# A pad of 224 bytes behind the resident tokens of a two-layer transformer trunk

## The chip, the cores and the metric

The kernel runs on one core of a Trainium2 chip, in one launch. The metric is the device time in microseconds (us), the median over several runs. Engines are named as in the profile: PE is TensorE's matrix product, PEld its weight load, DVE is VectorE, ACT is ScalarE, POOL is GpSimd, and SP is the engine that issues the DMAs.

## The reference

512 tokens of 1024 channels pass through two layers. Each layer is a half FFN, a mixer, and another half FFN, each followed by a residual sum and a layer norm. The even layer's mixer joins an RG-LRU and an mLSTM, the odd one's an RWKV-7 and a gated linear attention. All is float32.

```python
alpha = DEEPNORM_ALPHA
for l in range(DEPTH):
    x = layer_norm(alpha * x + 0.5 * swiglu_ffn(x, ffn1_wi[l], ffn1_wo[l]), ln_g[l, 0], ln_b[l, 0])
    mix = even_mixer(x, ...) if l % 2 == 0 else odd_mixer(x, ...)
    x = layer_norm(alpha * x + mix, ln_g[l, 1], ln_b[l, 1])
    x = layer_norm(alpha * x + 0.5 * swiglu_ffn(x, ffn2_wi[l], ffn2_wo[l]), ln_g[l, 2], ln_b[l, 2])
```

`swiglu_ffn` multiplies the tokens by a matrix of 1024 x 5632, takes silu of one half times the other half, and multiplies the 2816 results by a matrix of 2816 x 1024. The mixers begin with projections of the tokens and end with a product of 1024 x 1024.

## The kernel before, in words

**Precision.** TensorE multiplies float32r operands in one pass. To keep float32's accuracy each operand is split into a high and a low part, both exact in float32r, and each product is done as three: high x high, low x high, high x low. The tokens stay in memory as `xh` and `xl`, transposed (128 channels of a group on the partitions, eight groups of 512 tokens along them).

**Streamed weights.** All weights come once, as a list of chunks of 512 KB, 128 partitions x 1024 float32. `load` (line 81) issues a chunk's DMA on SP into one of two `raw` buffers. `split` (line 89) makes `whi` (ACT, line 97) and `wlo` (DVE, line 99), in two halves of 512 columns; both have five buffers. `weights` (line 107) hands out the next chunk and keeps two more split and two more loading.

**Three kinds of products**, each of 24 matmuls with 512 moving columns a chunk:

```python
# project_T_steps, 121, 122, 125: weights stationary, tokens moving
mm(o, hi[:, kt, :n], self.xh[:, kt, t0:t1], ...)
mm(o, hi[:, kt, :n], self.xl[:, kt, t0:t1], ...)
mm(o, lo[:, kt, :n], self.xh[:, kt, t0:t1], ...)
# project_N_steps, 145 to 147: tokens stationary, weights moving
mm(acc[t], self.xh[:, k, ts], hi[:, z, :], ...)
mm(acc[t], self.xl[:, k, ts], hi[:, z, :], ...)
mm(acc[t], self.xh[:, k, ts], lo[:, z, :], ...)
# out_mm, 154 to 156: left operand (ah, al) stationary, weights moving
mm(o, ah, hi[:, cs], ...)
mm(o, al, hi[:, cs], ...)
mm(o, ah, lo[:, cs], ...)
```

**An FFN** (`ffn`, line 206) runs in two parts, of 12 and 10 groups of inner channels. Each group takes two chunks of the first matrix (results `pgu`, by `project_T`); their gated product is split into `hh` and `hl`, the inner tiles. Then the group's rows of the second matrix come, one chunk a group: `out_mm` with `hh`, `hl` on the left, into `acc`, for four tiles of 128 tokens and two halves of the columns. So an FFN has 44 input chunks and 22 output chunks; there are four FFNs. The first five input chunks of an FFN run in two token halves of 256 columns (48 matmuls a chunk in place of 24), because the last tokens come late from the step before.

**The mixers** (`even`, line 307; `odd`, line 554) use the same chunks and functions. Results named `pqk`, `prg`, `pgg` and `pj` come from `project_T`, `pv` and the chunk products named `po` from `project_N`, `pout` from `out_mm` (class `MixOut`). Even: 16 column chunks (four of them in token halves), 8 row chunks, 8 output chunks, four of which have tiles `qk` on the left and four `xh` and `xl`. Odd: 17 column chunks (four in token halves), 8 row chunks, 8 output chunks, all with `xh` and `xl`. Each has one more narrow chunk, in halves and without its own low part (16 matmuls in each half). In the odd mixer the large products are queued in fixed portions between small ones (a list of counts, `FILL`, written by hand), and the small ones wait in turn for DVE and ACT.

**Where things lie.** Tiles are allocated along a partition in the order of their pools, each start a multiple of 32 bytes. The pools `cp` (tokens, identity), `wp` (weights), `lp` (small ones) and then the pool of the stage stack up from the left; `x` (the residual, 16,384 bytes) and the odd mixer's work tiles lie at the right end.

```python
self.cp = E(tc.tile_pool(name="cp", bufs=1))
self.wp = E(tc.tile_pool(name="wp", bufs=1))
self.lp = E(tc.tile_pool(name="lp", bufs=1))
...
self.xh = self.cp.tile([P, 8, S], F32R, name="xh")
self.xl = self.cp.tile([P, 8, S], F32R, name="xl")
self.ident = self.cp.tile([P, P], F32, name="ident")
```

| tile | first byte of the partition | modulo 256 |
|---|---|---|
| `xh`, `xl` (16,384 bytes each) | 16,512 and 32,896 | 128 |
| `ident` (512), then `expo` (4) | 49,280 and 49,792 | 128 |
| `raw` (2 x 4,096) | 49,824 | 160 |
| `whi`, `wlo` (5 x 4,096 each) | 58,016 and 78,496 | 160 |
| `hh`, `hl` (13 x 2,048 each) | 100,256 and 126,880 | 160 |
| even mixer's `qk` (8 x 2,048) | 121,600 | 0 |
| even mixer's `u`, `wbd` | 177,760 and 109,280 | 96 and 224 |

Inside these tiles matmul operands start at steps of 512 or 2,048 bytes, so the last column holds for all of them.

## Time and profile before

| what | value |
|---|---|
| median of three runs | 2075.99 us (2074.61, 2075.99, 2079.17) |
| profiled execution: span from its first to its last instruction | 2075.2 us |
| profiled execution: its own time | not listed apart from the span |
| mean granted TensorE clock | 0.993 |
| matmuls (passes) | 10,485 |
| the four FFNs' share of the span | about 1,480 us |
| even mixer, odd mixer | about 225 and 352 us |

How to read it: a line such as "PE 2054.0 (99%) x10485" gives an engine's busy time, its share of the span, and its instructions. Matmuls are pipelined and their ends are modelled: one is listed with a duration of about 390 ns while the next one starts some 230 ns after it. So PE's busy share and the mean of a group say little on what a matmul costs. The differences of starts, in the timeline or in the chain that ended last, say it.

### The profile page before, as it was taken

The numbers are of one execution on the slowest core, as the hardware profiler recorded it, in microseconds if no ns is written. First come the engines' busy times: TensorE is split into PE (matmuls) and PEld (weight loads), VectorE is DVE, ScalarE is ACT, GpSimd is POOL, SyncE is SP. The second block draws the span as 40 slices with busy tenths as digits, with TensorE's granted clock in tenths as the row PEclk, the third lists the DMA queues.
The fourth block names the chain that finished last, engine by engine and source line by source line (L and its number), as shares of the span: only waits on it lengthen the run. The fifth ranks groups of instructions, "written<-read, shape, count | busy, mean of one in ns | idle before, by whom it ended". The sixth has DMA issues, their size and how long they took to land.

```text
span 2075.2 us, 26007 instructions
## 1 busy us (share of the span) xinstructions
PE 2054.0 (99%) x10485; PEld 1681.6 (81%) x10485; DVE 998.2 (48%) x1850; ACT 692.0 (33%) x1214; POOL 69.2 (3%) x128
## 2 busy tenths in 40 slices
PE   9999999999999999999999999999999999999998
PEld 8888888876888888888888888887778788888886
DVE  4332333766783323336432333578768674323335
ACT  4322332556433322322332232156324333322320
POOL 0000000100010000000000000000010200000001
PEclk9999999999999999999999999999899999999999
DMA  5223232321233223222332332241302023233231
GB/s 174 92 92 122 92 98 85 97 94 67 62 102 112 91 92 122 92 92 71 112 98 95 112 102 92 77 157 36 102 31 72 1 82 112 92 101 112 94 99 61
DMA packets 56456, 191.42 MB, mean 92 GB/s; under 512 B 7488, under 2 KB 7952, under 8 KB 56336
## 3 DMA queue, kind: packets, MB, share of 16 engines
q1 hardware_dynamic: 56336, 189.77, 28.6%
q8 instruction: 82, 1.34, 0.3%
q14 instruction: 38, 0.31, 0.0%
HBM read 185.55 MB, written 4.19 MB: 91 GB/s over the span
## 4 chain that ended last, share of the span: by engine, by line
PE 94%; DVE 4%; ACT 1%; issue 1%; DMA 1%; POOL 0%; POOLq 0%; DVEq 0%; SPq 0%; ACTq 0%
PE pgu L121 16%; PE pgu L125 16%; PE pgu L122 16%; PE acc L154 8%; PE acc L155 8%; PE acc L156 8%; PE pout L155 1%; PE pout L154 1%; PE pj L121 1%; PE pout L156 1%; PE pj L122 1%; PE pj L125 1%; PE pst L167 1%; PE pv L145 1%; PE pv L147 1%; PE pv L146 1%
## 5 line engine op out<-in xcount | busy, mean ns | idle before, releaser
L99 DVE TENSOR_TENSOR wlo<-raw,whi 128x512 fp32r<-128x512 f32 x658 | 426.0, 686 | 557.8 <-ACT whi L97 526.0
L97 ACT ACTIVATE whi<-raw 128x512 fp32r<-128x512 f32 x661 | 379.6, 623 | 845.2 <-PE pgu L122 409.0
L122 PE MATMUL pgu<-xl,whi 128*128 128x512 f32 (+1 forms) x1568 | 571.5, 373 | 0.0
L121 PE MATMUL pgu<-xh,whi 128*128 128x512 f32 (+1 forms) x1568 | 570.0, 372 | 1.5 <-ACT whi L97 1.2
L125 PE MATMUL pgu<-xh,wlo 128*128 128x512 f32 (+1 forms) x1568 | 361.3, 372 | 0.0
L121 PEld LDWEIGHTS pgu<-xh,whi 128*128 128x128 f32 x1568 | 293.5, 188 | 58.2 <-ACT whi L97 1.6
L122 PEld LDWEIGHTS pgu<-xl,whi 128*128 128x128 f32 x1568 | 294.3, 188 | 57.0
L125 PEld LDWEIGHTS pgu<-xh,wlo 128*128 128x128 f32 x1568 | 275.4, 188 | 56.8
L154 PE MATMUL acc<-whi,hh 128*128 128x512 f32 x704 | 274.5, 390 | 0.0
L155 PE MATMUL acc<-whi,hl 128*128 128x512 f32 x704 | 274.2, 390 | 0.0
L156 PE MATMUL acc<-wlo,hh 128*128 128x512 f32 x704 | 272.3, 390 | 0.0
L232 DVE TENSOR_TENSOR sg<-sg,pgu 128x512 f32<-128x512 f32 (+1 forms) x96 | 61.7, 643 | 348.4 <-PE pgu L125 344.7
L156 PEld LDWEIGHTS acc<-wlo,hh 128*128 128x128 f32 x704 | 132.2, 188 | 27.4
L154 PEld LDWEIGHTS acc<-whi,hh 128*128 128x128 f32 x704 | 132.2, 188 | 27.3
L155 PEld LDWEIGHTS acc<-whi,hl 128*128 128x128 f32 x704 | 132.2, 188 | 27.1
L159 ACT ACTIVATE hh<-sg 128x512 fp32r<-128x512 f32 (+1 forms) x96 | 57.3, 597 | 125.0 <-DVE sg L232 124.9
L231 ACT ACTIVATE sg<-pgu 128x512 f32<-128x512 f32 (+1 forms) x96 | 53.8, 562 | 59.3 <-PE pgu L125 58.8
L189 POOL TENSOR_SCALAR rs<-mv 128x1 f32<-128x1 f32 x24 | 13.2, 549 | 1536.3 <-DVE mv L187 1536.3
L159 ACT ACTIVATE xh<-pst 128x512 fp32r<-128x512 f32 x48 | 27.8, 597 | 109.0 <-PE pst L167 108.9
L121 PE MATMUL pj<-xh,whi 128*128 128x512 f32 (+2 forms) x184 | 62.4, 358 | 0.0
L160 DVE TENSOR_TENSOR hl<-sg,hh 128x512 fp32r<-128x512 f32 (+1 forms) x96 | 61.4, 640 | 0.5 <-ACT hh L159 0.5
L122 PE MATMUL pj<-xl,whi 128*128 128x512 f32 (+2 forms) x184 | 60.8, 348 | 0.0
(333 smaller groups left out, 1999.0 us busy)
## 6 DMA issues: line engine op xcount, KB each, us to landing
raw<-ffn_wi SPq DMA_DIRECT2D x176, 512.0 KB, 3.5
raw<-ffn_wo SPq DMA_DIRECT2D x88, 512.0 KB, 3.5
raw<-od_krv SPq DMA_DIRECT2D x12, 512.0 KB, 3.6
raw<-ev_qk SPq DMA_DIRECT2D x8, 512.0 KB, 3.7
raw<-ev_rg SPq DMA_DIRECT2D x8, 512.0 KB, 3.4
raw<-ev_w_out SPq DMA_DIRECT2D x8, 512.0 KB, 3.5
raw<-od_w_out SPq DMA_DIRECT2D x8, 512.0 KB, 3.7
x<-x SPq DMA_DIRECT2D x4, 512.0 KB, 6.0
```

Of the source, the lines that this page charges most:

```text
L97: self.nc.scalar.activation(hi[:, sl], t[:, sl], AF.Copy)
L99: self.nc.vector.tensor_tensor(out=lo[:, sl], in0=t[:, sl], in1=hi[:, sl].bitcast(F32), op=ALU.subtract)
L121: mm(o, hi[:, kt, :n], self.xh[:, kt, t0:t1], start=kt == 0, stop=False)
L122: mm(o, hi[:, kt, :n], self.xl[:, kt, t0:t1], start=False, stop=lo is None and kt == 7)
L125: mm(o, lo[:, kt, :n], self.xh[:, kt, t0:t1], start=False, stop=kt == 7)
L154: mm(o, ah, hi[:, cs], start=first and i == 0, stop=False)
L155: mm(o, al, hi[:, cs], start=False, stop=False)
L156: mm(o, ah, lo[:, cs], start=False, stop=last and i == len(lhs) - 1)
L159: self.nc.scalar.activation(hi, src, AF.Copy)
L160: self.nc.vector.tensor_tensor(out=lo, in0=src, in1=hi.bitcast(F32), op=ALU.subtract)
L231: nc.scalar.activation(sg, pp[f, 0][:, t0:t1], AF.Silu)
L232: nc.vector.tensor_tensor(out=sg, in0=sg, in1=pp[u][:, t0:t1], op=ALU.mult)
```

## The change

One tile of 56 float32 (224 bytes a partition) is allocated behind the identity matrix. Nothing reads it or writes it. Everything allocated after it on the left moves up by 224 bytes: `expo`, `raw`, `whi`, `wlo`, the small tiles, and the tiles of the FFNs and mixers. The other lines of the diff blank out comments; line numbers behind the pad rise by two.

```diff
         self.ident = self.cp.tile([P, P], F32, name="ident")
         nc.sync.dma_start(self.ident, a["c_ident"])
+
+        self.cp.tile([P, 56], F32, name="pad")
         self.expo = self.cp.tile([P, 1], F32, name="expo")
...
```

## The prediction

> **What bounds the kernel now.** I read the page's head first (which engine), then the view by stage (where), then the chain of waits and the timeline inside single stages (what one matmul costs there).

> ```profile
> span 2075.2 us, 26007 instructions
> ...
> PE 94%; DVE 4%; ACT 1%; issue 1%; DMA 1%; POOL 0%; POOLq 0%; DVEq 0%; SPq 0%; ACTq 0%
> ```

> 94% of the chain that ended last is TensorE itself. By stage (length, then busy time of PE, PEld, DVE, ACT, POOL, then the granted clock, the DMA engines' share and GB/s): a stage of input products of an FFN, one of its output products, the even mixer, the odd mixer.

> ```profile
> 212.00:323.90 111.90, 111.90 (x482) 90.09 (x481) 38.47 (x61) 36.25 (x62) 0.00 (x0) 1.00 0.31 99
> 147.00:211.90 64.90, 64.90 (x288) 53.73 (x287) 20.15 (x31) 12.71 (x22) 0.00 (x0) 1.00 0.33 106
> 381.00:606.00 225.00, 222.00 (x1104) 176.46 (x1102) 163.31 (x331) 116.29 (x191) 11.29 (x19) 1.00 0.27 85
> 1347.00:1698.60 351.60, 345.09 (x2429) 275.30 (x2428) 257.90 (x593) 140.54 (x268) 35.83 (x72) 0.97 0.21 66
> ```

> In the FFN stages PE never rests, at a granted clock of 1.00; in the mixers it rests 3.0 and 6.5 us. So the time is the number of matmuls times the spacing of their starts, and a change that touches no instruction can only act on that spacing. "Mean ns of one" doesn't give it, because matmuls overlap; the starts do. The chain in an input stage (start, length, what), one piece per chunk of streamed weights:

> ```profile
> 215.97 1.87 PE pgu L125 x8
> 221.57 1.87 PE pgu L125 x8
> 227.17 1.87 PE pgu L125 x8
> ```

> The same eight matmuls come back every 5.60 us. A chunk is 24 matmuls of 512 columns (eight on each of lines 121, 122, 125), so one starts every 5.60 / 24 = 0.2333 us. The chain in an output stage, first and last of 54 pieces:

> ```profile
> 159.88 0.23 PE acc L154
> ...
> 171.89 0.23 PE acc L156
> ```

> (171.89 − 159.88) / 53 = 0.2266 us. Both are single-pass products of 128 rows, 128 columns of weights and 512 moving columns, with PE never idle, yet one is 6.7 ns shorter. The timeline of the even mixer tells what doesn't make the difference: the output product there is the same function as the FFN's (lines 154 to 156), with other left operands.

> ```profile
> 583.79 0.39 PE L154 MATMUL pout<-whi,xh 128*128 128x512 f32 x1
> ...
> 586.35 0.39 PE L156 MATMUL pout<-wlo,xh 128*128 128x512 f32 x1
> ...
> 587.25 0.40 PE L155 MATMUL pout<-whi,qk 128*128 128x512 f32 x1
> 587.49 0.39 PE L156 MATMUL pout<-wlo,qk 128*128 128x512 f32 x1
> 587.72 0.39 PE L154 MATMUL pout<-whi,xh 128*128 128x512 f32 x1
> ...
> 594.89 0.39 PE L154 MATMUL pout<-whi,qk 128*128 128x512 f32 x1
> 595.12 0.39 PE L155 MATMUL pout<-whi,qk 128*128 128x512 f32 x1
> 595.35 0.39 PE L156 MATMUL pout<-wlo,qk 128*128 128x512 f32 x1
> 595.58 0.39 PE L154 MATMUL pout<-whi,xh 128*128 128x512 f32 x1
> ```

> Twelve products with the tokens as left operand: (586.35 − 583.79) / 11 = 0.2327 us. Five steps with `qk` tiles: (0.47 + 0.69) / 5 = 0.232 us. Same line order, same shapes, same streamed right operand as `acc`, but the slower spacing. What is left is where the operands lie. Modulo 256 bytes, by the program's allocation: tokens 128, streamed weights 160, the FFN's inner tiles 160, the `qk` tiles 0. The pairs (moving, stationary) are then: `pgu` (128, 160) 0.233; `pout` with tokens (160, 128) 0.233; `pout` with `qk` (160, 0) 0.232; `acc` (160, 160) 0.2266. Only where both lie at the same place is the product short. Every tile starts at a multiple of 32 bytes, so the trace can't say whether 64, 128 or 256 is the true period; the change brings the distance to 0 in all of them.

> **The change part by part.** It adds one tile that nobody reads or writes, so no instruction, DMA, wait or queue place is added or moved. Everything that is allocated behind the identity matrix on the left side moves up 224 bytes: weights and inner tiles come to 160 + 224 = 384, that is 128 modulo 256, as the tokens. `x` and the odd mixer's work tiles, at the right end, stay.

> 1. FFN input products of 512 columns, from (128, 160) to (128, 128). A short FFN chunk is 24 x 0.2266 = 5.44 us, so 0.16 us less. Each FFN has 44 such chunks, of which 5 run in halves; 4 x 39 = 156 chunks x 0.16 = 25.0 us. PE is the only engine on that path, so all of it counts.
> 2. The same in halves (256 columns): 4 x 5 x 48 = 960 matmuls. No row shows one with both operands at one place. The chain at the start of the first FFN has eight of them, then eight transposes of 128 columns, which load as many weights:

> ```profile
> 15.12 0.95 PE pgu L125 x8
> 16.07 0.87 PE pst L167 x8
> ```

> 0.95 / 8 = 119 ns against 0.87 / 8 = 109 ns. The transposes stream half the columns, so 109 looks like the time of a weight load, and a half product won't go below it: at most 10 ns to gain, at least none (a loss is excluded as far as the rule of the 512-column rows holds). I take 5 ns, the middle, since the nearest rows give 3.4 by share (6.7 / 233 of 119) and 6.7 by matmul: 960 x 5 = 4.8 us, bounds 0 and 9.6.
> 3. Mixers. Whole chunks with tokens on one side: even 12 + 8 (columns and rows of the projections) + 4 (output) = 24, x 0.16 = 3.8 us; odd 13 + 8 + 8 = 29, x 0.16 = 4.6 us. In halves 448 matmuls x 5 ns = 2.2 us. Here small products wait on VectorE and ScalarE in between, and what PE saves can come back as a wait (VectorE is busy 258 of the odd mixer's 352 us). Since PE rests only 9.5 us in both, most should be kept: I take four fifths of 10.6 = 8.5 us; bounds a third of the 8.4 alone, 2.8, and all of it with 10 ns for the halves, 12.9.
> 4. FFN output products go from (160, 160) to (128, 128): distance 0 before and after, nothing. The even mixer's `qk` operands move with the weights, (160, 0) to (128, 224), the same distance: nothing.
> 5. What hides under the faster chunk: its two halves' splitting and the next load.

> ```profile
> L99 DVE TENSOR_TENSOR wlo<-raw,whi 128x512 fp32r<-128x512 f32 x658 | 426.0, 686 | 557.8 <-ACT whi L97 526.0
> L97 ACT ACTIVATE whi<-raw 128x512 fp32r<-128x512 f32 x661 | 379.6, 623 | 845.2 <-PE pgu L122 409.0
> ...
> raw<-ffn_wi SPq DMA_DIRECT2D x176, 512.0 KB, 3.5
> ```

> Per chunk ScalarE needs 2 x 0.623 = 1.25 us, VectorE 2 x 0.686 = 1.37 us, the DMA 3.5 us, against 5.44 us: still covered. These read and write tiles that all move together, so their cost is taken as unchanged; if ScalarE and VectorE lost that cover, they would cost up to 2.6 us a chunk.

> Sum: 25.0 + 4.8 + 8.5 = 38.3 us. The trace's span of 2075.2 would become 2036.9; it lies 0.8 us below the median of the three runs, 2075.99, which would become 2037.7 us.

> [...]

> **The rivals.**
> - *Nothing changes*, 2076.0 us: the shortness of `acc` has another reason, such as higher address bits or which tiles those are. For it: there is a single kind of short pair, and one kernel. Against it: `pout` shares code, shapes and right operand with `acc`, and its `qk` tiles lie in the same stretch of memory as the inner tiles. [...]
> - *Slower*: each operand pays by its own place, and a start at a multiple of 64 bytes (128, 0) is the dear one, 160 the cheap one. The four pairs fit this too: `acc` has no dear operand, the others one. Then everything lies dear afterwards: 156 + 53 chunks pay a second 0.16 us, 33.4 us, and the 88 output chunks of the FFNs pay two, 28.2 us: 2137.6 us. It decides as soon as `acc` is spaced over 0.2266 us. Against it: products of float32 in two passes, whose operands lie at (0, 0) for `pS` and at (96, 224) for `pgr`, take the same busy time.

> ```profile
> L414 PE MATMUL pS<-qk 128*128 128x512 f32 x8 | 4.1, 599 | 0.0
> L469 PE MATMUL pgi<-u,wbd 128*128 128x512 f32 x8 | 4.1, 592 | 0.0
> L468 PE MATMUL pgr<-u,wbd 128*128 128x512 f32 x8 | 4.1, 591 | 0.0
> ```

>   Four pairs of passes in 4.1 us each way: a start at 0 isn't dear there. These run at half the pace, so it is a hint only.
> - *The chunk becomes bound elsewhere*: excluded above in the FFNs; in the mixers it takes away at most the 10.6 us, 2046.

> **How the numbers follow.** Equal places are cheap: 0.83. Nothing changes: 0.09. Dear multiples of 64: 0.08. The first case's ends: 25.0 + 9.6 + 12.9 = 47.5 us saved, 2028.5, less the 1.4 by which the fastest run lies below the median (2074.61), 2027; and 25.0 + 0 + 2.8 = 27.8 saved, 2048.2, plus the 3.2 of the slowest run (2079.17), 2051. About 0.97 of that case lies inside, 0.80 of all, so the range needn't reach to the others. No change here means within 0.2%, 4.2 us, about what a measurement can tell: faster 0.83, same 0.09, slower 0.08, straight from the three cases.

> **What would show it.** Right: `pgu` chunks every 5.44 us in the chain, `pout` and `pj` with tokens at about 0.227 us, `acc` still 0.2266, `pout` with `qk` still 0.232, half products between 109 and 119 ns, and PE's rests in the mixers a few us longer. Wrong: chunks still at 5.60 (no change), or `acc` above 0.2266 and `pgu` near 0.240 (the slower rival). The size would be off if the half products gave nothing, or if the odd mixer's small products simply waited for VectorE longer.

## The result, and the profile after

The changed kernel took 2053.15 us (median of five runs, 2048.92 to 2058.12), the kernel before 2078.06 us (five runs, 2074.61 to 2079.17): 0.988 of the time, with a 95% interval of 0.9865 to 0.9895. It is faster, by 24.9 us where 38.3 were forecast; the median lies 2 us above the forecast range. The profiled execution took 2053.15 us. Its span is 2051.4, 23.8 us less than the span of before.

The view by stage, for the stages shown of before (FFN input products, FFN output products, even mixer, odd mixer; the same columns):

```profile
209.20:318.10 108.90, 108.90 (x482) 90.22 (x481) 38.43 (x61) 36.12 (x62) 0.00 (x0) 1.00 0.34 102
143.90:209.00 65.10, 65.10 (x289) 53.93 (x288) 20.16 (x31) 12.70 (x22) 0.00 (x0) 1.00 0.33 105
375.00:600.60 225.60, 222.23 (x1107) 178.33 (x1106) 163.66 (x332) 116.31 (x191) 11.27 (x19) 0.99 0.28 85
1329.70:1680.90 351.20, 345.40 (x2428) 277.72 (x2427) 257.40 (x591) 140.76 (x268) 35.73 (x72) 0.96 0.21 65
```

Only the FFN's input stage is shorter, 108.9 us against 111.9. The output stage is as it was, and so is each mixer: 225.6 against 225.0 us, 351.2 against 351.6. The whole gain comes from the FFNs. In the mixers the granted clock is a hundredth lower (0.99 and 0.96, from 1.00 and 0.97).

The chain in an input stage, one piece per chunk (start, length, what), and in an output stage, first and last of 54 pieces:

```profile
310.89 1.81 PE pgu L127 x8
316.33 1.81 PE pgu L127 x8
```

```profile
159.93 0.23 PE acc L157
...
171.94 0.23 PE acc L156
```

A chunk takes 5.44 us, or 226.7 ns a product, from 233.3; `acc` stays at (171.94 − 159.93) / 53 = 226.6 ns. The halves, in the chain at the start of the first FFN:

```profile
14.95 0.96 PE pgu L127 x8
15.91 0.87 PE pst L169 x8
```

They became slower: 0.96 / 8 = 120 ns. Over all undisturbed starts of `pgu`'s half products in the two traces the mean spacings are 118.4 ns before and 119.9 ns after.

### The profile page after: what moved, and what is told of

It is laid out like the page before. It is cut to its first block, busy times and chain, and to the rows that moved or that the text cites. A ratio compares the mean times of both kernels' runs of the same rounds, so it can differ in the third digit from the quotient of the medians.

```text
span 2051.4 us, 26007 instructions
## 1 busy us (share of the span) xinstructions
PE 2030.7 (99%) x10485; PEld 1686.5 (82%) x10485; DVE 998.3 (49%) x1850; ACT 692.0 (34%) x1214; POOL 69.1 (3%) x128
## 4 chain that ended last, share of the span: by engine, by line
PE 92%; DVE 5%; ACT 1%; issue 1%; DMA 1%; POOL 0%; POOLq 0%; DVEq 0%; SPq 0%; ACTq 0%
PE pgu L123 16%; PE pgu L124 16%; PE pgu L127 16%; PE acc L158 8%; PE acc L156 8%; PE acc L157 8%; PE pout L156 1%; PE pout L157 1%; PE pout L158 1%; PE pj L123 1%; PE pj L124 1%; PE pst L169 1%; DVE wlo L101 1%; PE pj L127 1%; DVE ZU L781 1%; DVE ZU L780 1%
## 5 line engine op out<-in xcount | busy, mean ns | idle before, releaser
L99 ACT ACTIVATE whi<-raw 128x512 fp32r<-128x512 f32 x661 | 379.5, 623 | 833.4 <-PE pgu L124 400.8
L123 PE MATMUL pgu<-xh,whi 128*128 128x512 f32 (+1 forms) x1568 | 563.1, 368 | 1.5 <-ACT whi L99 1.2
L124 PE MATMUL pgu<-xl,whi 128*128 128x512 f32 (+1 forms) x1568 | 564.0, 368 | 0.0
L127 PE MATMUL pgu<-xh,wlo 128*128 128x512 f32 (+1 forms) x1568 | 353.6, 367 | 0.0
L156 PE MATMUL acc<-whi,hh 128*128 128x512 f32 x704 | 274.4, 390 | 0.0
L156 PEld LDWEIGHTS acc<-whi,hh 128*128 128x128 f32 x704 | 132.2, 188 | 27.1
L161 ACT ACTIVATE xh<-pst 128x512 fp32r<-128x512 f32 x48 | 27.8, 597 | 107.9 <-PE pst L169 107.9
## 6 DMA issues: line engine op xcount, KB each, us to landing
raw<-ffn_wi SPq DMA_DIRECT2D x176, 512.0 KB, 3.5
raw<-ffn_wo SPq DMA_DIRECT2D x88, 512.0 KB, 3.5
raw<-od_krv SPq DMA_DIRECT2D x12, 512.0 KB, 3.6
raw<-ev_qk SPq DMA_DIRECT2D x8, 512.0 KB, 3.6
raw<-ev_rg SPq DMA_DIRECT2D x8, 512.0 KB, 3.5
raw<-ev_w_out SPq DMA_DIRECT2D x8, 512.0 KB, 3.5
raw<-od_w_out SPq DMA_DIRECT2D x8, 512.0 KB, 4.0
x<-x SPq DMA_DIRECT2D x4, 512.0 KB, 5.8
```

Source lines behind the costliest of these rows:

```text
L99: self.nc.scalar.activation(hi[:, sl], t[:, sl], AF.Copy)
L123: mm(o, hi[:, kt, :n], self.xh[:, kt, t0:t1], start=kt == 0, stop=False)
L124: mm(o, hi[:, kt, :n], self.xl[:, kt, t0:t1], start=False, stop=lo is None and kt == 7)
L127: mm(o, lo[:, kt, :n], self.xh[:, kt, t0:t1], start=False, stop=kt == 7)
L156: mm(o, ah, hi[:, cs], start=first and i == 0, stop=False)
L161: self.nc.scalar.activation(hi, src, AF.Copy)
```

## The experiments

The experiments answer three questions: is it the distance of the two operands, which distance, and why not in the mixers? In 1 to 3 each kernel ran once, so the spacings, means over hundreds or thousands of products, carry the argument, and the times only go with them. A product's spacing is the time from its start to the next one's.

**1. The inner tiles alone out of place** (`inner_off`), added to the changed kernel:

```diff
         self.nc.vector.memset(z, 0.0)
+        self.lp.tile([P, 8], F32, name="pad3")
```

> The pad behind the tokens as in the changed kernel, and 32 bytes more ahead of the FFN's inner tiles: tokens and weights at 128 modulo 256, inner tiles at 160. Theory (the distance between the moving and the stationary operand decides): pgu keeps the 226.7 ns spacing of the changed kernel, a chunk every 5.44 us; acc, now 32 bytes apart, goes from 226.7 to 233.3 ns, and its 88 chunks cost 0.16 us each: 14 us above the changed kernel, about 2067 us. Rival (acc is short for a reason of its own, not for its places): acc stays at 226.7 ns and the time at about 2053 us.

Measured: 2069.9 us, span 2068.1. The chain in the output stage, first and last of 52 pieces, then two chunks of an input stage:

```profile
159.89 0.23 PE acc L158
...
171.79 0.23 PE acc L158
```

```profile
835.48 1.81 PE pgu L127 x8
840.92 1.81 PE pgu L127 x8
```

`acc` now takes (171.79 − 159.89) / 51 = 233.3 ns, while `pgu` keeps 5.44 us a chunk. Moving one operand by 32 bytes switches each kind of product on its own, so the places decide, and nothing else about `acc`. The time is 16.8 us above the changed kernel's median where 14 were expected; its mean clock was 0.989, the changed kernel's 0.991 (experiment 4 has the price). Together with the unchanged `acc` at (128, 128) this also rules out the slower rival of the prediction, by which each operand's own place would count.

**2. Other distances.** Only the sizes and places of the pads differ from the kernel before; in `d16_d48`, `d240` and `d8` the tokens also start some bytes inside a longer tile, for instance

```diff
-        self.xh = self.cp.tile([P, 8, S], F32R, name="xh")
+        self.xh = self.cp.tile([P, 8 * S + 64], F32R, name="xh")[:, 4:4 + 8 * S].rearrange("p (a b) -> p a b", a=8)
```

First with two distances in one kernel, for `whi` and for `wlo`:

> Tokens and inner tiles at 128 modulo 256, whi at 192 (64 bytes on), wlo at 0 (128 bytes on). Theory with a period of 64 bytes: both distances act like 0, so the products on whi and on wlo are spaced by 226.7 ns in pgu and in acc, and the time is that of the changed kernel, about 2053 us. Theory with a period of 128: whi's products at 233.3, wlo's at 226.7 ns. Theory with a period of 256: 233.3 ns everywhere, acc too, 14 us above the kernel before, about 2092 us. None of them expects a spacing under 226.7 ns; one would mean that 0 is not the best distance.

> The tokens start 16 bytes further on, at 144 modulo 256; whi lies at 160 (16 bytes on), wlo and the inner tiles at 192 (48 bytes on). Theory (only distances that are a multiple of 64 are short): pgu at 233.3 ns on whi and on wlo; acc at 233.3 on whi (32 bytes from the inner tiles) and short on wlo (same place). About 2085 to 2090 us. Rival (what counts is the 32-byte step an operand lies in): whi's pgu products, 16 bytes apart in one step of 32 or the next, split from wlo's, one of the two at 226.7 ns.

> Tokens at 128 modulo 256, whi at 64 (192 bytes on), wlo and the inner tiles at 96 (224 bytes on). Theory with a period of 64 bytes: pgu's products on whi at 226.7 ns, on wlo at 233.3, a chunk every 16 x 0.2267 + 8 x 0.2333 = 5.49 us; acc at 233.3 on whi and 226.7 on wlo where its neighbours allow it. Theories with a period of 128 or 256: whi's pgu products at 233.3 too, 5.60 us a chunk.

They took 2088.1, 2084.2 and 2077.6 us. None of the split outcomes came out cleanly. In `pgu`, means over all starts: 233.2 ns on `whi` at 64 and 232.0 on `wlo` at 128; 233.6 at 16 and 230.8 at 48; 229.3 at 192 and 233.0 at 224. `acc` in `d64_d128`, at distances 192 and 128, took 232.0, so that kernel comes nearest to a period of 256. And in the last two kernels `acc`'s products on `wlo`, at distance 0 but alone between two at 32, took 231.1 and 230.7 ns in place of 226.7. So a product's spacing hangs on its neighbours too (experiment 3 has more on that), and the distances had to be tried one at a time:

> A pad of 32 bytes in place of 224: all weights and inner tiles 64 bytes past the tokens modulo 256, so that no product of another distance stands between. Acc stays at distance 0. Theory with a period of 256 (the mixed run gave 233.2 ns at 64): pgu at about 233 ns, a chunk every 5.60 us, about 2076 us. Theory with a period of 64, which needs unbroken runs to show: 226.7 ns and about 2053 us. The half products, 120 ns at distance 0 and 118.4 at 32, were 115.3 at 64 in the mixed run and should be about 114 here under both.

> A pad of 96 bytes: weights and inner tiles 128 bytes past the tokens. Theory with a period of 256: pgu above 230 ns (the mixed run gave 232.0), about 2070 us or more. Theory with a period of 128 or 64 that only unbroken runs show: 226.7 ns, about 2053 us.

> A pad of 160 bytes: weights and inner tiles 192 bytes past the tokens, that is 64 ahead of them. The mixed run gave 229.3 ns on these, with 226 in the lower half. Theory (a product settles at its distance's own spacing only in an unbroken run): pgu at 226 to 227 ns here, about 2053 to 2056 us, so that 0 isn't the only short distance. Rival (the mean of the mixed run is its own spacing): 229.3 ns, 15 us less than before, about 2061 us.

> The pad of 224 bytes, and the tokens moved 16 bytes on, so that weights and inner tiles lie 16 bytes ahead of the tokens modulo 256 (distance 240). Theory (exactly equal places are needed): pgu at about 233 ns, a chunk every 5.60 us, about 2076 us. Rival (a neighbourhood of 0 on the side of 192, which gave 229.0 ns, is short, or shorter): 226.7 ns or less, 2053 us or less.

> The pad of 224 bytes, and the tokens moved so that weights and inner tiles lie 8 bytes past them modulo 256. Theory (exactly equal places are needed): pgu at about 233 ns, about 2076 us. Rival (a few bytes on either side don't matter): 226.7 ns, about 2053 us.

They took 2073.1, 2078.9, 2061.0, 2071.6 and 2075.8 us (the kernel before beside them: 2075.8, and 2078.5 for the last two). Chunks in the chains of the input stages, for distance 64, 192 and 8:

```profile
267.31 1.87 PE pgu L126 x8
272.91 1.87 PE pgu L126 x8
```

```profile
1078.61 1.83 PE pgu L126 x8
1084.10 1.83 PE pgu L126 x8
```

```profile
816.05 1.88 PE pgu L126 x8
821.67 1.88 PE pgu L126 x8
```

5.60, 5.49 and 5.62 us a chunk. Mean spacing of `pgu` over all starts of each trace, by distance from tokens to weights modulo 256 (the whole chunk at one distance; where two figures stand, they are those on `whi` and on `wlo`; `acc` was at 0 and 226.7 to 227.0 ns in all of them):

| distance, bytes | 0 | 8 | 32 | 64 | 128 | 192 | 240 |
|---|---|---|---|---|---|---|---|
| 512 columns, ns | 226.7 | 231.9 to 234.7 | 233.3 | 233.3 | 233.0 | 228.6 to 229.1 | 231.7 |
| 256 columns, ns | 119.9 | 120.0 | 118.4 | 115.7 | 118.6 | 117.8 | 116.5 |

Periods of 64 and 128 bytes are out. So is one of 512: in the kernels before and after, the operands of all the short products lie an odd multiple of 256 bytes apart, but by the sizes of its tiles `half64` (experiment 4) has `wlo` 124 x 512 bytes behind `xh`, and `pgu` takes 226.6 ns on it. 0 is the best tried for whole products, and 8 bytes off on one side or 16 on the other is enough to lose it; 192 keeps two thirds of the gain, as the rival of `u192` had it (2061 us), not the theory. For half products 0 is nearly the worst. One thing these runs can't tell apart: a product's own two operands, or its moving operand and the weights of the next product, whose load begins with it (in the kernel before, the product at 175.13 us and the load for the next one start together). In every unmixed kernel both pairs lie at the same distance.

**3. Breaks in the run of products** (`cut_after`), on the changed kernel:

```diff
+            if cut and kt in (3, 7):
+                self.nc.tensor.transpose(self.psum("cut", "C")[:, :P], self.ident, self.ident)
...
-                    self.project_T(pp[u], ws[u], t0, t1)
+                    self.project_T(pp[u], ws[u], t0, t1, cut=t1 - t0 == S)
```

> The changed kernel with one transposition of the identity matrix (never read) after every eight products of an FFN's whole input chunks, 468 of them. Theory (after a break the spacing starts at about 232 ns whatever the places, and falls to 226.7 from the tenth product on; this is why the mixers gained less): with a break every eight products pgu's spacing between breaks means 229 to 231 ns, first steps about 232. Rival (the mixers' products are slower because VectorE and ScalarE read and write more there): pgu stays at 226.7 ns between the breaks. The time is of no use here: the breaks themselves cost some 468 x 0.15 to 0.3 us, 70 to 140 us.

Measured: 2120.3 us, and a mean of 230.3 ns over the 2,940 `pgu` starts between breaks, `pgu` being at distance 0 throughout. The timeline behind one break (start, length, what):

```profile
64.94 0.27 PE L125 MATMUL cut<-ident 128*128 128x128 f32 x1
64.97 0.47 PE L122 MATMUL pgu<-xh,whi 128*128 128x512 f32 x1
65.28 0.39 PE L123 MATMUL pgu<-xl,whi 128*128 128x512 f32 x1
65.51 0.40 PE L122 MATMUL pgu<-xh,whi 128*128 128x512 f32 x1
65.74 0.40 PE L123 MATMUL pgu<-xl,whi 128*128 128x512 f32 x1
65.98 0.39 PE L122 MATMUL pgu<-xh,whi 128*128 128x512 f32 x1
```

From the second product on, (65.98 − 65.28) / 3 = 233 ns. Over all breaks the second, third and fourth spacings average 231.6, 231.9 and 232.4 ns, and the fifth 227.0: the way down is not even. Spacing by spacing, products at distance 0 go through one series, here from a run of `pv` and `prg` in the even mixer of the changed kernel (457.11 to 460.09 us): 229, 233, 236, 224, 231, 236, 228, 233, 231, and from there 226 to 227 ns. Other runs enter the series further on, and a few are at 227 at once. So the short spacing is not a property of one product. It sets in within some ten products, and most breaks cost it again, in the FFN as in the mixers; the mixers' traffic isn't needed for that. The profile of before held the same opening, in `acc`, where four transpositions cut the run:

```profile
374.87 0.39 PE L154 MATMUL acc<-whi,hh 128*128 128x512 f32 x1
...
376.26 0.39 PE L154 MATMUL acc<-whi,hh 128*128 128x512 f32 x1
...
378.53 0.39 PE L155 MATMUL acc<-whi,hl 128*128 128x512 f32 x1
```

The first six spacings shown average (376.26 − 374.87) / 6 = 231.7 ns, the next ten (378.53 − 376.26) / 10 = 227. The 54 pieces that the prediction read lie inside a run without a break.

**4. The clock, and the halves moved to 64.** The changed kernel again, and one in which the `hi` part of the chunks that run in halves lies 64 bytes further on:

```diff
-        hi = self.wp.tile([P, 1024], F32R, name="whi", bufs=NSLOT)
+        hi = self.wp.tile([P, 1088], F32R, name="whi", bufs=NSLOT)
+        hi = hi[:, 16:1040] if self.nsp in self.halved else hi[:, :1024]
```

> The changed kernel once more, beside runs of the kernel before, for the granted clock of each run. Theory (part of the mixers' saving was lost because more stretches at half clock fell into the profiled run): over the runs the time falls as the mean clock rises, some 2 us for each 0.001, in both kernels, and the clocks of the two kernels overlap; at equal clock the difference is 25 to 28 us. Rival (the change itself lowers the clock): every run of the changed kernel is granted less than every run of before.

> The changed kernel, with whi's buffers 256 bytes longer and the hi part of those chunks that run in token halves (28 of them) written 64 bytes further on. Their products on whi, 119.8 ns at distance 0, were 115.3 to 115.8 at distance 64 in the runs with 64; 28 x 32 = 896 of them, 4 ns each: 3.6 us less than the changed kernel at equal clock, with whole products still at 226.7. Rival (the half products on wlo, which stay at distance 0, keep the pace up or the buffers' new places cost elsewhere): no difference that the clock's spread lets see.

The changed kernel took 2054.84 us (0.9887 of before, interval 0.9863 to 0.991), `half64` 2053.47 us (0.9881, 0.9861 to 0.99): no difference between the two that the runs let see. In its trace the half products on `whi` took 117.3 ns, from 119.8, not 115.5: 896 x 2.5 ns = 2.2 us, which the clock's spread covers. No version tried clearly beats the changed kernel.

On the clock: ten executions of before have spans of 2072.9 to 2080.0 us at mean granted clocks of 0.990 to 0.994, nine of the changed kernel 2047.1 to 2056.3 us at 0.989 to 0.993. A fit with one slope for both gives 1.7 us for each 0.001 and 25.5 us between the kernels at equal clock. The ranges overlap, so a change that always lowers the clock is out; but the means are 0.9921 and 0.9909, which is worth 2 us. Part of that shift may come with the change, by one wait in the even mixer (next section, step 3); the rest stays open.

## Why the prediction was right in kind and too large

The mechanism held: the distance of the operands sets the spacing (whole products in an FFN: 226.7 ns at 0, 233.3 at 32 bytes). Two terms failed: the half products were bounded at no loss and lost, and the mixers' products were priced as in an FFN, at an unchanged clock. By the prediction's own steps, in the two profiled traces (differences of the starts of the same product in both):

1. *FFN input products of 512 columns, 25.0 us.* Right: 24.8 us over 3,744 products, 233.3 to 226.7 ns. Experiment 1 shows the cause as it was put, the distance.
2. *FFN halves, +4.8 us.* Wrong in sign: 1.4 us lost. The step that failed is "a loss is excluded as far as the rule of the 512-column rows holds". The rule doesn't hold for 256 columns: in the table the order of the distances is another one, and 0 is among the worst (119.9 ns, against 115.7 at 64). The measured loss lies outside the bounds of 0 and 9.6 us. That the 109 ns of a transpose are the time of a weight load was the author's estimate from one row; no run shows it.
3. *Mixers, 8.5 us.* They gave nothing: even −0.2, odd +0.2. Four things replace "four fifths":
   - The whole products gave 2.1 us in the even and 3.2 in the odd mixer, 5.3 of 8.4. The step assumed that a product costs there what it costs in an FFN. Experiment 3 shows what was missing: behind most breaks the products start at some 232 ns in either kernel. In the mixers, by position after the last break, the mean spacing in the changed kernel is 231.8, 232.9 and 231.9 ns for the first three, about 228 for the seventh to ninth, and about 227 from the tenth on; before, it is between 231 and 234 at every position. The row of `pout` that the forecast expected at 227 shows both cases (transpositions and three products with `qk` stand ahead of the second run of twelve products with tokens, from 581.99 on):

```profile
577.87 0.39 PE L158 MATMUL pout<-wlo,qk 128*128 128x512 f32 x1
578.10 0.40 PE L156 MATMUL pout<-whi,xh 128*128 128x512 f32 x1
...
579.03 0.40 PE L157 MATMUL pout<-whi,xl 128*128 128x512 f32 x1
...
581.99 0.39 PE L156 MATMUL pout<-whi,xh 128*128 128x512 f32 x1
...
584.49 0.39 PE L158 MATMUL pout<-wlo,xh 128*128 128x512 f32 x1
```

   One run starts at (579.03 − 578.10) / 4 = 232.5 ns. The later one is at (584.49 − 581.99) / 11 = 227.3 from its first product on, so not each break costs the short spacing; why this one did not stays open.
   - The halves lost 0.6 us there, where 1.8 had been counted as gained.
   - Longer waits and the small products took another 0.5 us.
   - Stretches at half clock took 4.2 us more. The forecast held the mixers' clock fixed. In the even mixer a stretch of the changed kernel has no counterpart in the profile of before (first the changed kernel, with the 3.4 us ahead of the stretch, then the same products before):

```profile
415.00:418.40 3.40, 1.49 (x9) 0.94 (x9) 3.40 (x7) 1.33 (x3) 0.00 (x0) 1.00 0.51 154
418.40:421.80 3.40, 3.40 (x10) 2.60 (x9) 3.40 (x8) 3.37 (x7) 0.00 (x0) 0.50 0.49 154
```

```profile
425.00:429.00 4.00, 4.00 (x19) 3.23 (x18) 3.97 (x9) 3.99 (x9) 0.00 (x0) 1.00 0.32 128
```

   Ten products fit into 3.4 us where 19 fitted into 4.0. The timeline of the changed kernel, just behind a wait of PE for VectorE:

```profile
417.74 0.47 PE L123 MATMUL pqk<-xh,whi 128*128 128x512 f32 x1 [1.91 <-DVE qk L307]
...
419.02 0.63 PE L123 MATMUL pqk<-xh,whi 128*128 128x512 f32 x1
419.45 0.63 PE L124 MATMUL pqk<-xl,whi 128*128 128x512 f32 x1
419.87 0.63 PE L123 MATMUL pqk<-xh,whi 128*128 128x512 f32 x1
```

   427 ns a product: 1.5 us lost in the even mixer. Ahead of the stretch PE rested for 3.40 − 1.49 = 1.91 us. Before, the same wait was there, 1.76 us long, without such a stretch. The fourteen kept traces tell when it comes. Within a trace the stretches at half clock lie on a grid of 3.413 us: in this one, those from 418.40 and from 1425.34 us are 295 steps apart. In seven traces 1.91 to 2.01 us of this wait fall into one step of the grid, and half clock follows in the next step: the changed kernel both times, `half64`, `inner_off`, `cut_after`, `d192_d224` and `u192`. In the other seven at most 1.69 us fall into one step, and none follows. Before, the grid cuts the wait into 0.49 and 1.27 us, in `u64` a wait of 2.14 into 0.91 and 1.23. So in these traces it went by two things at this place, the length of the wait, 1.91 us in the changed kernel and 1.76 before, and where the grid lies in an execution.

   In the odd mixer, around the same small products, first before, then the changed kernel:

```profile
1590.00:1604.00 14.00, 14.00 (x175) 11.59 (x172) 7.76 (x13) 6.52 (x12) 0.00 (x0) 0.76 0.18 43
```

```profile
1568.00:1583.00 15.00, 15.00 (x147) 12.41 (x148) 6.66 (x9) 4.72 (x8) 0.00 (x0) 0.54 0.11 36
```

   A granted clock of 0.76 over 14 us is 6.7 us at half rate, 0.54 over 15 us is 13.8: twice as long, and with the other stretches 2.7 us lost.
4. *`acc` and `pout` with `qk`: nothing.* Right: 226.8 before and 226.7 ns after, and 244.1 and 244.0 ns (with their breaks).
5. *Splitting and loading stay covered.* Right: PE is busy throughout the FFN stages, with the faster chunk too (108.90 of 108.90 us in the input stage, 65.10 of 65.10 in the output stage).

The sum 25.0 + 4.8 + 8.5 thus became 24.8 − 1.4 − 0.0, with 0.4 from other products of the FFNs: 23.8 us. The range failed with it, since both of its ends took the halves and the mixers as gains or nothing. In the profiled run the stretches at half clock alone took 4.2 us; without them the saving would have been 28.0 us, just above the 27.8 of the range's slow end. The fastest run of the changed kernel, at a clock of 0.993, lies inside the range (2048.92 us).

In experiment 1, products alike in everything but 32 bytes differ by 6.6 ns. What waits for what inside is not shown by any run here. Nor is what sets off half clock; step 3 has what the traces show of it, in the changed kernel 1.91 us of rest inside one step of 3.413 us and a granted clock of 0.50 in the next.

## What to carry to other kernels

Where TensorE never rests, read the spacing of starts rather than durations, and compare groups of equal products: a few ns between them (here 6.6), times thousands (here 3,744), are worth the search for the one thing that differs, here the operands' places modulo 256 bytes. Look for the first products of a run as well as for its middle. Don't carry a spacing from an unbroken stage to a stage with breaks (here 226.7 ns became some 232 behind most breaks), nor from one product size to another (here 6.6 ns less became 1.5 more), without a row of that stage; bound such a term from below zero too. And where a mixed stage has stretches at half clock, hold a saving of a few us there against what they take: here 5.3 us of whole products in the mixers stood against 4.2 us more at half clock.
